# Layer 0's latent attention units in two groups of six and four key tiles

## Chip, core and metric

The kernel runs on one core of a Trainium2 chip. The metric is the device time of one execution in microseconds (us). Every time below comes from runs of the kernel before, or from one profiled execution of it. The engines are named as the profile names them: PE (TensorE, matrix products; PEld is its loading of weights), DVE (VectorE), ACT (ScalarE), POOL (GpSimd) and SP (SyncE, which here issues DMAs).

## What is computed

Two attention layers run over 1024 latent tokens and 256 context tokens of width 1024. Layer 0 is grouped-query attention with 16 query heads of width 64 over 4 key and value heads; layer 1 is a latent attention. The change touches layer 0 alone:

```python
def gqa_attend(q, k, v):
    s = jnp.einsum('bqhgd,bkhd->bhgqk', q, k).astype(jnp.float32) * (GQA_HEAD_DIM ** -0.5)
    p = jax.nn.softmax(s, axis=-1).astype(v.dtype)
    return jnp.einsum('bhgqk,bkhd->bqhgd', p, v)
...
    k_all = jnp.concatenate([kc, k], axis=1)
    v_all = jnp.concatenate([vc, v], axis=1)
    o = sweep_query_blocks(lambda qb: gqa_attend(qb, k_all, v_all), q).reshape(B, S, GQA_WIDTH)
...
    oc = gqa_attend(qc, kc, vc).reshape(B, L, GQA_WIDTH)
```

Latent queries read all 1280 keys (ten tiles of 128), context queries only the 256 context keys (two tiles).

## The kernel before

**Units.** `Attention.run` walks over a list of units. A latent unit is one query head with its 1024 latent queries against ten key tiles. A context unit is one key head with its four query heads of 256 context queries against the last two key tiles. Layer 0 has 20 units, counted from 0 here: latent ones, with context units at places 4, 9, 18 and 19. Unit 17 is the last latent one.

**A unit.** For each key tile, `scores_by_halves` (L492) multiplies keys by queries in two halves of 512 queries, which run side by side in the two halves of PE's rows. A tile is four products per half: high part by high part, low by high, high by low, and a product with the constant `minus` that subtracts a shift of each query (`shift`). The scores go to a PSUM buffer `st`, of which there are two. ACT takes the exponential (L508) into `p`, a pair of tiles to a buffer, five buffers in all, just those of one unit. Then `do_av` (L546) multiplies all value tiles by the exponentials into the one PSUM buffer `av`, and `finish` copies it to `os` on ACT (L576).

**Sums for the softmax.** The exponentials of a unit are added up over its tiles. POOL adds whole tiles (`acp`, L542). DVE first adds the two tiles of a pair for the last two pairs (`pair_sum`, `acd`, L528), which POOL adds on top. The `total` of a unit (L597, products with `twos`) sums over the partitions on PE; DVE transposes and inverts it (L601, L602). It is put on a list and runs one unit later, ahead of that unit's value products. The reciprocals go out to memory and come back spread over partitions (`rrow`, `rb`), POOL multiplies them with the gate (L616) and the result with both (L617), and `od` is stored.

**The shift.** Each query's shift is the maximum over its approximate scores. These maxima are made units ahead: with every score tile two steps of maxima are issued, products on PE (L393, L403) into one of three PSUM buffers `mx`, and reduces on DVE (L395, L404). A latent unit has 20 such steps, the last four for the context keys. 28 steps are done when unit 0 starts, so in most latent units the last step for the next latent unit falls on the sixth tile. Then DVE reduces once more (L416), and a `turn` is put on a list: PE transposes the row (L422), DVE copies it to `crow` (L424), and SP copies it into `shift` by DMA (L427). `run_turns` issues what is on this list, before the change once per unit, behind its tenth score tile.

**Order.** PE, DVE and ACT run in the order in which the code issues (`manual_schedule` in `run`). POOL and SP are put in order by the compiler's scheduler, each a queue that runs in its order. The weights for the output projection are loaded in pieces, one behind every second unit, with casts on ACT (L157) and subtractions on POOL (L136, `wb`).

**The groups.** A group is a run of key tiles whose scores are issued together and whose value products follow. `cut` is zero for all units but the last latent one, so a unit is one group there:

```python
                    cut = 6 if u is self.last_lat else 0
                    ...
                    for group in (kts[:cut], kts[cut:]):
                        ...
                        self.run_turns()
                        ...
                        while self.totals:
                            self.totals.pop(0)()
                        ...
                        self.do_av(u, group, ps)
```

Of the kernel before, what the change touches and what calls it, by code (L numbers as in the profile page):

```python
# [36 lines left out]
def hybrid_kernel(ctx: ExitStack, tc: tile.TileContext, ins: dict, out: bass.AP):  # L37
# [197 lines left out]
    class Plan:  # L235
# [8 lines left out]
        def run(self):  # L244
            engines = mybir.EngineType
            with tc.manual_schedule(engines={engines.PE, engines.Activation, engines.DVE, engines.Pool, engines.SP}):
                for _, _, fn, args in sorted(self.todo, key=lambda e: e[:2]):
                    fn(*args)
# [60 lines left out]
    class Attention:  # L309
# [319 lines left out]
        def run(self, lead, ahead, extra, tail):  # L629

            count = lead
            parts = None
            with tc.manual_schedule(engines={mybir.EngineType.PE, mybir.EngineType.DVE, mybir.EngineType.Activation}):
                for t, u in enumerate(self.units):
                    kts = u["kts"]
                    for v in self.units[t:t + 2]:
                        self.load_v(v)
                    while self.started < min(t + 1 + ahead, len(self.units)):
                        self.start_unit()
                    whole = len(kts) > 4  # L640
                    cut = 6 if u is self.last_lat else 0

                    def one_more():
                        nonlocal count
                        count += 1
                        self.maxima(count, t + 1 + ahead)

                    for group in (kts[:cut], kts[cut:]):
                        if not group:
                            continue  # L650
                        end = group[-1] == kts[-1]
                        final = t == len(self.units) - 1 and end
                        p2s = [self.pp.tile([P, 2, 1024], F32, name="p", tag="p", bufs=5) for _ in range(len(group) // 2)]
                        ps = [p2[:, a, :] for p2 in p2s for a in range(2)]

                        late = not whole and t >= len(self.units) - 2
                        n1 = len(ps) - (4 if whole and end else 2 if late else 0)
                        for i, kt in enumerate(group):
                            self.run_deferred(self.step)
                            if HALVES[self.l]:  # L660
                                count += 2
                                self.scores_by_halves(u, kt, ps[i], self.next_maxima(count, t + 1 + ahead))
                            else:
                                self.do_scores(u, kt, ps[i], one_more)
                            self.step += 1
                            if i < n1:
                                self.add_up(u, [ps[i]], [])
                        if end and t + 2 < self.started:
                            self.state[id(self.units[t + 2])].pop("rest", lambda: None)()
                        if final:  # L670
                            tail()
                        self.run_turns()
                        if late or final:
                            self.add_up(u, [], ps[n1:])
                        elif n1 < len(ps):
                            sums = [self.pair_sum(p2) for p2 in p2s[n1 // 2:]]
                            self.add_up(u, *(([], sums) if cut else (sums, [])))
                        if final:
                            self.run_deferred(self.step + 2)
                        while self.totals:  # L680
                            self.totals.pop(0)()
                        if t % 2 and end:
                            if parts:
                                parts()
                            parts = extra.pop(0)() if extra else None
                        self.do_av(u, group, ps)
                        self.step += (2 + len(group)) // 3
                while self.totals:
                    self.totals.pop(0)()
            self.run_deferred(self.step)  # L690
# [600 lines left out]
    units = []  # L1291
# [8 lines left out]
    for g, pos in ((0, 4), (1, 9), (3, 18), (2, 19)):  # L1300
        units.insert(pos, ctxu[g])

    at = Attention(0, units, dict(scale=0.125, load=l0_load, scores=l0_scores, maxima=l0_maxima, mparts=1, open=l0_open, kbufs=2, qbufs=3, vw=256))
    stE = ExitStack()
    with tc.tile_pool(name="wkg0a", bufs=4, **right) as wkg:
        for m in range(2, 4):
# [286 lines left out]
    units = []  # L1593
    for p_ in range(8):
        for par in range(2):
            h = 2 * p_ + par
            units.append(dict(kind="lat", h=h, pair=p_, par=par, vg=(h // 4, 128 * (h // 2 % 2)), vc=64 * par,
                              kts=list(range(TT))))
    at = Attention(1, units, dict(scale=float(96 ** -0.5), load=l1_load, scores=l1_scores, maxima=l1_maxima, mparts=2, open=l1_open, open_late=l1_open_late,
                                  kbufs=3, qbufs=3, vw=128))  # L1600
    stE = ExitStack()

# [197 lines left out]
```

## Time and profile before

| | |
|---|---|
| median of 3 runs | 1709.44 us (1705.8 to 1714.31) |
| the profiled execution | 1707.59 us, of which the span of the program is 1705.8 |
| granted clock of PE, mean | 0.996 |
| attention of layer 0 | from about 372 to 752 us of the span |
| attention of layer 1 | from about 1197 to 1616 us |

The span is cut into 40 slices in the page; each digit is the busy share of a slice in tenths:

```profile
PE   8999999999999999999989999999999999999998
DVE  3765552357778777625675657754677777777231
ACT  4642221124445544432244533340434444344310
POOL 2763431218789988743245544350668787787511
PEclk9999999999999999999999999999999999999999
```

A slice is 42.6 us, so the attention of layer 0 fills the tenth to the eighteenth. The costliest groups of instructions that the change touches, with busy time, the mean length of one in ns, the idle time of the engine before them, and what ended it:

```profile
L508 ACT ACTIVATE p<-st 128x1024 f32<-128x1024 f32 x328 | 336.0, 1027 | 169.8 <-PE st L501 134.8
L542 POOL TENSOR_TENSOR acp<-acp,p 128x1024 f32<-128x1024 f32 x128 | 305.8, 2389 | 7.8
L555 PE MATMUL av<-p,v 128*64 128x512 f32 x1312 | 289.9, 595 | 0.0
L528 DVE TENSOR_REDUCE acd<-p 128x512 f32<-128x1024 f32 x124 | 144.7, 1220 | 7.9 <-ACT p L508 7.8
```

These counts are of both layers; layer 1 has units of the same shape.

### The profile page before, as it was taken

The numbers are of one execution on the slowest core, as the hardware profiler recorded it, in microseconds if no ns is written. First come the engines' busy times: TensorE is split into PE (matmuls) and PEld (weight loads), VectorE is DVE, ScalarE is ACT, GpSimd is POOL, SyncE is SP. The second block draws the span as 40 slices with busy tenths as digits, with TensorE's granted clock in tenths as the row PEclk, the third lists the DMA queues.
The fourth block names the chain that finished last, engine by engine and source line by source line (L and its number), as shares of the span: only waits on it lengthen the run. The fifth ranks groups of instructions, "written<-read, shape, count | busy, mean of one in ns | idle before, by whom it ended". The sixth has DMA issues, their size and how long they took to land. (4 is left out here: it accounts for less than half of the span.)

```text
span 1705.8 us, 27449 instructions
## 1 busy us (share of the span) xinstructions
PE 1667.9 (98%) x10244; PEld 1196.9 (70%) x10244; DVE 1046.6 (61%) x1807; ACT 645.1 (38%) x943; POOL 961.4 (56%) x646
## 2 busy tenths in 40 slices
PE   8999999999999999999989999999999999999998
PEld 5776778775555555557878898986767667667587
DVE  3765552357778777625675657754677777777231
ACT  4642221124445544432244533340434444344310
POOL 2763431218789988743245544350668787787511
PEclk9999999999999999999999999999999999999999
DMA  9557754521242422146433766766565655653452
GB/s 315 169 150 241 253 176 142 152 81 45 63 121 61 112 63 63 38 137 204 139 94 117 233 189 182 207 192 164 135 137 134 134 122 121 146 124 91 125 160 74
DMA packets 219821, 238.97 MB, mean 140 GB/s; under 512 B 23016, under 2 KB 159192, under 8 KB 219688
## 3 DMA queue, kind: packets, MB, share of 16 engines
q1 hardware_dynamic: 219264, 237.11, 49.5%
q8 instruction: 81, 1.33, 0.3%
q14 instruction: 52, 0.43, 0.1%
q10 hardware_dynamic: 424, 0.11, 0.0%
HBM read 163.37 MB, written 73.63 MB: 139 GB/s over the span
## 5 line engine op out<-in xcount | busy, mean ns | idle before, releaser
L395 DVE TENSOR_REDUCE m<-mx 128x1 f32<-128x512 f32 x512 | 336.2, 687 | 176.3 <-PE mx L393 170.5
L508 ACT ACTIVATE p<-st 128x1024 f32<-128x1024 f32 x328 | 336.0, 1027 | 169.8 <-PE st L501 134.8
L542 POOL TENSOR_TENSOR acp<-acp,p 128x1024 f32<-128x1024 f32 x128 | 305.8, 2389 | 7.8
L555 PE MATMUL av<-p,v 128*64 128x512 f32 x1312 | 289.9, 595 | 0.0
L555 PEld LDWEIGHTS av<-p,v 128*64 128x64 f32 x1312 | 90.9, 137 | 180.6 <-issue 177.9
L542 POOL TENSOR_TENSOR acp<-p 128x1024 f32<-128x1024 f32 x34 | 81.4, 2396 | 148.0 <-ACT p L508 147.9
L542 POOL TENSOR_TENSOR acp<-acp,acd 128x1024 f32<-128x1024 f32 x60 | 142.2, 2370 | 22.3 <-DVE acd L528 19.1
L528 DVE TENSOR_REDUCE acd<-p 128x512 f32<-128x1024 f32 x124 | 144.7, 1220 | 7.9 <-ACT p L508 7.8
L136 POOL TENSOR_TENSOR wb<-wraw,wa 128x512 fp32r<-128x512 f32 (+3 forms) x73 | 95.4, 1326 | 81.2 <-ACT wa L157 81.2
L93 PE MATMUL mm<-wa,hh 128*128 128x512 f32 (+2 forms) x336 | 127.4, 379 | 1.1 <-ACT hh L890 1.1
L501 PE MATMUL st<-QH,KH 64*128 64x512 f32 x320 | 122.2, 404 | 1.0 <-DVE gth L303 1.0
L95 PE MATMUL mm<-wa,hl 128*128 128x512 f32 (+2 forms) x336 | 121.5, 362 | 1.6 <-DVE hl L893 1.6
L94 PE MATMUL mm<-wb,hh 128*128 128x512 f32 (+2 forms) x336 | 121.2, 361 | 0.0
L501 PE MATMUL st<-QH,KL 64*128 64x512 f32 x320 | 119.0, 392 | 0.0
L501 PE MATMUL st<-QL,KH 64*128 64x512 f32 x320 | 118.3, 390 | 0.0
L576 ACT COPY os<-av 128x512 f32<-128x512 f32 x36 | 21.1, 587 | 255.9 <-PE av L555 205.9
L93 PE MATMUL y<-wa,oh 128*128 128x512 f32 (+1 forms) x296 | 114.1, 386 | 1.4 <-DVE yt L750 1.4
L95 PE MATMUL y<-wa,ol 128*128 128x512 f32 (+1 forms) x296 | 113.5, 384 | 0.0
L94 PE MATMUL y<-wb,oh 128*128 128x512 f32 (+1 forms) x296 | 113.5, 383 | 0.0
L404 DVE TENSOR_REDUCE m<-mx 128x2 f32<-128x512 f32 x144 | 95.4, 688 | 24.0 <-PE mx L403 18.9
L393 PE MATMUL mx<-KH,QH 64*128 64x512 f32 x256 | 102.7, 405 | 0.5 <-DVE m L404 0.3
L93 PE MATMUL mm<-hh,wa 128*128 128x512 f32 x256 | 102.0, 399 | 0.5 <-ACT th L86 0.5
(240 smaller groups left out, 4023.1 us busy)
## 6 DMA issues: line engine op xcount, KB each, us to landing
mraw<-in_l_w_mod SPq DMA_DIRECT2D x64, 256.0 KB
wraw<-in_l_w_in SPq DMA_DIRECT2D x28, 512.0 KB
KH<-k1h SPq DMA_DIRECT2D x32, 320.0 KB
KL<-k1l SPq DMA_DIRECT2D x32, 320.0 KB
rb<-rrow SPq DMA_DIRECT2D x72, 128.0 KB
mraw<-in_l_w_mod SPq DMA_DIRECT2D x16, 512.0 KB
sgd<-gth SPq DMA_DIRECT2D x32, 256.0 KB
wraw<-in_l_w_out SPq DMA_DIRECT2D x16, 512.0 KB
```

The lines of the kernel that those rows point to most:

```text
L93: pe.matmul(ps, lhsT=lh(k), rhs=rh(k), start=first and i == 0, stop=False)
L94: pe.matmul(ps, lhsT=lh(k), rhs=rl(k), start=False, stop=False)
L95: pe.matmul(ps, lhsT=ll(k), rhs=rh(k), start=False, stop=last and i == len(ks) - 1)
L136: eng.tensor_sub(lo, a, b)
L393: pe.matmul(held["m"][:, cs], lhsT=q[:, t * P:(t + 1) * P], rhs=k[:, ks], start=j == 0, stop=j == len(pairs) - 1)
L395: dve.reduce_max(s["m"][:, i, n:n + 1], held["m"], axis=AX.X)
L404: dve.reduce_max(s["m"][:, 2 * i:2 * i + 2, 2 if u["kind"] == "lat" else 0], m.rearrange("p (a b) -> p a b", a=2), axis=AX.X)
L501: pe.matmul(ps[:, n * 512:(n + 1) * 512], lhsT=lh, rhs=rh, start=j == 0, stop=j == last)
L508: act.activation(p, ps, AF.Exp, scale=self.ops["scale"])
L528: dve.reduce_sum(t[:, ns], p2.rearrange("p a n -> p n a")[:, ns, :], axis=AX.X)
L542: pool.tensor_add(t, a, b)
L555: pe.matmul(s["av"][64 * n:64 * n + 64, :], lhsT=s["v"][:, kt, u["vc"]:u["vc"] + 64], rhs=p[:, n * 512:(n + 1) * 512], start=kt == kts[0], ...
```

## The change

`Attention` takes a number `cut` with its operations, 6 for layer 0 and 0 for layer 1. Every latent unit of layer 0 but the last is then issued as two groups, tiles 0 to 5 and tiles 6 to 9: scores, values, scores, values. In each of the two groups the last pair of exponentials is summed by DVE (`n1 = len(ps) - 2`) and handed on to POOL as a part; before, it was the last two pairs of the unit. The totals of earlier units are issued only in a unit's second group. The last latent unit, the context units and layer 1 keep what they had. Turns are still issued behind every group.

```diff
-                    cut = 6 if u is self.last_lat else 0
+                    lastl = u is self.last_lat
+                    cut = 6 if lastl else self.ops["cut"] if whole else 0
...
-                        n1 = len(ps) - (4 if whole and end else 2 if late else 0)
+                        if cut and not lastl:
+                            n1 = len(ps) - 2
+                        else:
+                            n1 = len(ps) - (4 if whole and end else 2 if late else 0)
...
-                            self.add_up(u, *(([], sums) if cut else (sums, [])))
+                            self.add_up(u, *(([], sums) if lastl else (sums, [])))
...
-                        while self.totals:
+                        while self.totals and (end or lastl):
...
-    at = Attention(0, units, dict(scale=0.125, load=l0_load, scores=l0_scores, maxima=l0_maxima, mparts=1, open=l0_open, kbufs=2, qbufs=3, vw=256))
+    at = Attention(0, units, dict(scale=0.125, load=l0_load, scores=l0_scores, maxima=l0_maxima, mparts=1, open=l0_open, cut=6, kbufs=2, qbufs=3, vw=256))
...
-    at = Attention(1, units, dict(scale=float(96 ** -0.5), load=l1_load, scores=l1_scores, maxima=l1_maxima, mparts=2, open=l1_open, open_late=l1_open_late,
+    at = Attention(1, units, dict(scale=float(96 ** -0.5), load=l1_load, scores=l1_scores, maxima=l1_maxima, mparts=2, open=l1_open, cut=0, open_late=l1_open_late,
```

The order of PE in unit 1 before, from the last context maximum of the sixth tile to the seventh tile, and at the unit's end:

```order
L403 MATMUL mx<-KA,QH 128x256 x2
L501 MATMUL st<-QL,KA 128x512
L501 MATMUL st<-shift_2949,minus 128x512
L501 MATMUL st<-QL,KA 128x512
L501 MATMUL st<-shift_2949,minus 128x512
L393 MATMUL mx<-KA,QH 128x512
L501 MATMUL st<-QH,KA 128x512 x2
```

```order
L393 MATMUL mx<-KA,QH 128x512
L501 MATMUL st<-QL,KA 128x512 x2
L501 MATMUL st<-shift_2949,minus 128x512 x2
L422 MATMUL mx<-ident,m_3829 8x128
L597 MATMUL mx<-acp,twos 32x256 x4
L555 MATMUL av<-p,v 64x512 x20
```

The same two places with the change:

```order
L403 MATMUL mx<-KA,QH 128x256 x2
L501 MATMUL st<-QL,KA 128x512
L501 MATMUL st<-shift_2949,minus 128x512
L501 MATMUL st<-QL,KA 128x512
L501 MATMUL st<-shift_2949,minus 128x512
L422 MATMUL mx<-ident,m_3826 8x128
L555 MATMUL av<-p,v 64x512 x12
L393 MATMUL mx<-KA,QH 128x512
L501 MATMUL st<-QH,KA 128x512 x2
```

```order
L393 MATMUL mx<-KA,QH 128x512
L501 MATMUL st<-QL,KA 128x512 x2
L501 MATMUL st<-shift_2949,minus 128x512 x2
L597 MATMUL mx<-acp,twos 32x256 x4
L555 MATMUL av<-p,v 64x512 x8
```

The turn (L422) has moved from behind the tenth tile to behind the sixth, and twelve of the twenty value products (L555) with it; the total (L597) still stands behind the tenth. Such a place is found in 13 units; in units 3 and 8 the turn stays at the unit's end.

DVE in the same unit, from the first maxima of the unit to the reciprocal, before:

```order
L395 TENSOR_REDUCE m<-mx 128x1 x8
L404 TENSOR_REDUCE m<-mx 128x2 x4
L416 TENSOR_REDUCE m_3829<-m 128x8
L395 TENSOR_REDUCE m<-mx 128x1 x8
L424 CAST crow<-mx 8x128
L528 TENSOR_REDUCE acd<-p 128x512 x4
L601 STREAM_TRANSPOSE mx<-mx 128x256
L602 RECIPROCAL cr<-mx 128x8
```

and with the change:

```order
L395 TENSOR_REDUCE m<-mx 128x1 x8
L404 TENSOR_REDUCE m<-mx 128x2 x4
L416 TENSOR_REDUCE m_3826<-m 128x8
L424 CAST crow<-mx 8x128
L528 TENSOR_REDUCE acd<-p 128x512 x2
L395 TENSOR_REDUCE m<-mx 128x1 x8
L528 TENSOR_REDUCE acd<-p 128x512 x2
L601 STREAM_TRANSPOSE mx<-mx 128x256
L602 RECIPROCAL cr<-mx 128x8
```

The copy of the turn now follows L416 directly, and half of the pair sums stands ahead of the last eight maxima.

POOL in unit 3 and into the context unit behind it, before:

```order
L542 TENSOR_TENSOR acp<-p 128x1024
L616 TENSOR_TENSOR rb<-rb,sg 128x512
L617 TENSOR_TENSOR os<-os,rb 128x512
L542 TENSOR_TENSOR acp<-acp,p 128x1024 x4
L136 TENSOR_TENSOR wb<-wraw,wa 128x512 x2
L542 TENSOR_TENSOR acp<-acp,acd 128x1024 x2
L616 TENSOR_TENSOR rb<-rb,sg 128x512
```

and with the change:

```order
L616 TENSOR_TENSOR rb<-rb,sg 128x512
L542 TENSOR_TENSOR acp<-p 128x1024
L617 TENSOR_TENSOR os<-os,rb 128x512
L542 TENSOR_TENSOR acp<-acp,p 128x1024 x2
L542 TENSOR_TENSOR acp<-acp,acd 128x1024
L542 TENSOR_TENSOR acp<-acp,p 128x1024 x2
L136 TENSOR_TENSOR wb<-wraw,wa 128x512 x2
L542 TENSOR_TENSOR acp<-acp,acd 128x1024
```

The product with the reciprocals (L616) now stands ahead of the unit's first add, and the weight pieces (L136) ahead of its last one only.

## The prediction

> **What bounds the kernel now.** I read the page first, then the stretch that the change touches.
>
> ```profile
> span 1705.8 us, 27449 instructions
> PE 1667.9 (98%) x10244; PEld 1196.9 (70%) x10244; DVE 1046.6 (61%) x1807; ACT 645.1 (38%) x943; POOL 961.4 (56%) x646
> ```
>
> PE is busy for 98% of the span. The windows view of the attention of layer 0 (371 to 753 us), and of 8 us inside it, agrees; its columns are length, busy time by engine, granted clock, DMA share and GB/s.
>
> ```profile
> core 0: us, PE busy (x) PEld busy (x) DVE busy (x) ACT busy (x) POOL busy (x), PEclk, DMA share, GB/s
> 371.00:753.00 382.00, 379.28 (x2617) 210.18 (x2616) 280.57 (x442) 189.53 (x199) 319.39 (x155) 1.00 0.28 75
> 460.00:468.00 8.00, 7.30 (x56) 3.68 (x51) 4.12 (x8) 3.23 (x4) 4.79 (x3) 1.00 0.35 100
> ```
>
> PE is idle for 2.7 of 382 us. A change that only reorders PE's own work has almost nothing to win there, and every new wait that lands on PE is paid in full. The timeline of one latent unit on PE (number 5, counted from 0) shows what a unit is made of. Columns: start, length, engine, line, operation, names, sizes, count.
>
> ```profile
> 466.50 0.50 PE L393 MATMUL mx<-KA,QH 64*128 64x512 f32 x1
> 467.77 0.61 PE L501 MATMUL st<-QH,KA 64*128 64x512 f32 x2
> 469.14 0.50 PE L501 MATMUL st<-QH,KA 64*128 64x512 f32 x2
> ...
> 473.00 0.39 PE L501 MATMUL st<-QH,KA 64*128 64x512 f32 x2
> ...
> 473.58 0.28 PE L403 MATMUL mx<-KA,QH 64*128 64x256 f32 x1
> ...
> 478.18 0.39 PE L501 MATMUL st<-QH,KA 64*128 64x512 f32 x2
> ...
> 479.43 0.27 PE L422 MATMUL mx<-ident,m 128*8 128x128 f32 x1
> 479.63 0.64 PE L597 MATMUL mx<-acp,twos 128*32 128x256 f32 x8
> 480.20 8.80 PE L555 MATMUL av<-p,v 128*64 128x512 f32 x40
> 488.94 0.50 PE L393 MATMUL mx<-KA,QH 64*128 64x512 f32 x1
> ```
>
> Ten score tiles take 12.93 us (466.50 to 479.43), the transpose of the next shift (L422, "the turn") 0.20, the total of the unit before (L597) 0.57, the ten value tiles 8.74; a unit is 22.44 us. The last tile, from its first score product at 478.18 to the turn, takes 1.25. The sixth tile starts at 473.00, so with nothing to wait for, a turn could stand behind it at 474.25.
>
> DVE in the same unit, and ACT's last two exponentials of it:
>
> ```profile
> 467.04 4.98 DVE L395 TENSOR_REDUCE m<-mx 128x1 f32<-128x512 f32 x8 [1.56 <-PE mx L393]
> 471.94 2.68 DVE L404 TENSOR_REDUCE m<-mx 128x2 f32<-128x512 f32 x4
> 474.65 0.18 DVE L416 TENSOR_REDUCE m<-m 128x8 f32<-128x24 f32 x1
> ...
> 479.95 4.68 DVE L528 TENSOR_REDUCE acd<-p 128x512 f32<-128x1024 f32 x4
> 484.56 0.44 DVE L601 STREAM_TRANSPOSE mx<-mx 128x256 f32<-128x256 f32 x1
> 485.04 0.21 DVE L602 RECIPROCAL cr<-mx 128x8 f32<-128x8 f32 x1
> ```
>
> ```profile
> 478.44 2.12 ACT L508 ACTIVATE p<-st 128x1024 f32<-128x1024 f32 x2 [0.46 <-PE mx L393]
> ```
>
> L416 makes the row that the turn transposes. It ends at 474.83, which is 4.6 us before the turn needs it now, and 0.58 after the end of the sixth tile.
>
> **The change, part by part.** First, the turn moves into a wait. The list of pending turns is run behind each group. In 13 of the 15 changed units (all but 3 and 8, where by the program's order L416 follows later tiles) the turn therefore stands behind the sixth tile, and the value products of group one stand behind it in PE's order. Nothing on DVE ahead of L416 changes, so it still ends 8.33 us after the unit's start. What it takes to hand over to PE I read from a total that waited for an add of Pool:
>
> ```profile
> 459.19 4.82 POOL L542 TENSOR_TENSOR acp<-acp,acd 128x1024 f32<-128x1024 f32 x2
> 464.07 0.64 PE L597 MATMUL mx<-acp,twos 128*32 128x256 f32 x8 [0.70 <-POOL acp L542]
> ```
>
> The add ended at 464.01 and PE started 0.06 later. For DVE I take 0.1, between 0.05 and 0.2. PE thus stands 0.58 + 0.1 = 0.68 us at the end of group one. At the unit's end nothing is won for it: the turn started there without a wait on PE, and its 0.20 only moves. Behind the waiting turn stand twelve value products and then the second scores, for which ACT, DVE and Pool wait in turn.
>
> Second, the value products come in two runs. The last latent unit is cut 6 + 4 already:
>
> ```profile
> 727.29 5.37 PE L555 MATMUL av<-p,v 128*64 128x512 f32 x24
> 732.59 0.50 PE L501 MATMUL st<-QH,KA 64*128 64x512 f32 x2
> ...
> 737.00 3.65 PE L555 MATMUL av<-p,v 128*64 128x512 f32 x16
> 740.59 0.50 PE L501 MATMUL st<-QH,KA 64*128 64x512 f32 x2
> ```
>
> From each start to the next scores it takes 5.30 and 3.59 us, together 8.89 against 8.74: +0.15 for one more end of a run.
>
> Third, the score pipeline starts once more per unit. PE writes scores into two PSUM buffers that ACT must empty. The waits view of the attention of layer 0 (total, times, longest):
>
> ```profile
> PEld st L501 <- ACT p L508: 22.6, 67, 0.7
> ...
> PE st L501 <- ACT p L508: 0.8, 3, 0.3
> ...
> POOL rb L616 <- DMA rb<-rrow: 27.3, 9, 4.7
> ```
>
> The weight loads wait 67 times, 0.34 us each, some four times per unit. PE itself hardly waits: tile 1 lasts from 467.77 to 469.14, which is 1.37 with such a wait behind it, and the last tile 1.25 without. A wait costs PE about 0.1, not 0.34. A group starts with both buffers free, so I expect two waits in six tiles and one in four, three for four. Ten tiles were 12.93; six are 7.75 (473.00 - 466.50 + 1.25), and four 5.14 (tile 3 starts one tile of 1.25 behind the 2.64 of the first two, and then 1.25): 12.89, a gain of 0.04.
>
> A changed unit: 0.68 + 0.15 - 0.04 = +0.79, 13 times that is +10.3. Units 3 and 8 have only the other two terms, +0.11 each, +0.2.
>
> Fourth, the pair sums: two per unit before and after, and seven adds on Pool. DVE's sum of tiles 4 and 5 falls into the first value run. Its exponential ends about 1.1 us behind the sixth tile (480.56 against 479.43 at the unit's end), the sum takes half of 4.68, and the run lasts 5.30. The sum of 8 and 9 and the reciprocal (0.44, 0.21) end 4.3 us behind the scores; the next unit's first maximum reaches DVE 0.57 + 3.59 + 0.54 = 4.7 us behind them. So these cost nothing, with 0.4 to spare; were that cover gone, each unit would lose the difference.
>
> Fifth, the shift's copy leaves earlier. In unit 6, PE waited for it:
>
> ```profile
> 490.40 0.68 PE L501 MATMUL st<-shift,minus 64*128 64x512 f32 x2 [0.27 <-DMA shift<-crow]
> ...
> 492.26 0.51 PE L501 MATMUL st<-QH,KA 64*128 64x512 f32 x2
> ```
>
> Tile 2 starts 3.32 us after the unit there, and 2.64 in unit 5. The copy now leaves half a unit earlier; the stores and loads ahead of it on SP wait for Pool's L617 until some 10 us into the unit, and 13 are left then: -0.7.
>
> Sixth, the context units. Units 4 and 9 are two tiles long, and the total of the unit before stands close behind them. Pool decides there:
>
> ```profile
> 620.23 0.64 PE L597 MATMUL mx<-acp,twos 128*32 128x256 f32 x8
> ...
> 630.97 1.29 POOL L616 TENSOR_TENSOR rb<-rb,sg 128x512 f32<-128x512 f32 x1 [2.91 <-DMA rb<-rrow]
> ...
> 633.59 2.40 POOL L542 TENSOR_TENSOR acp<-p 128x1024 f32<-128x1024 f32 x1
> 636.07 9.77 POOL L542 TENSOR_TENSOR acp<-acp,p 128x1024 f32<-128x1024 f32 x4
> ...
> 456.74 2.50 POOL L136 TENSOR_TENSOR wb<-wraw,wa 128x512 fp32r<-128x512 f32 x2
> ```
>
> The reciprocals come back to Pool (L616) 10.7 us behind a total. With the shorter pair sum it is 9.4, and the next unit now starts 4.16 behind the total instead of 9.31, so L616 moves from 1.4 to 5.2 us into a unit. From there L616 and L617 (2.6), six adds (14.7), in unit 3 the two weight pieces (2.5) and the last add (2.4) end at 27.4. The total in unit 4 could start at 22.55 + 2.6 = 25.2. It waits 2.2, against 0.70 before: +1.5, between 0 and +5 by the time of that DMA. Unit 8 has no weight pieces ahead of its last add and just fits: 0.
>
> The sum is 10.3 + 0.2 - 0.7 + 1.5 = +11.3 us. The profiled execution took 1707.59 us (1.8 of it around the span), 1.85 under the median of 1709.44. From the one I get 1718.9, from the other 1720.7, and take 1720.
>
> **The rivals.** The score pipeline pays it back: if each wait of the weight loads is worth its 0.34 to PE, the one that goes gives 15 x 0.34 = 5.1, and +6 is left: 1715.5, inside 0.5% (8.5 us, about what a measurement of this kernel can tell from no change). For it speaks the row of 22.6 us, against it the row of 0.8.
>
> Faster, at the same place: ACT catches up in both pauses, so that only two of 4.2 waits stay in each unit (15 x 2.2 x 0.34 = -11.2), and the turn does not stand. With -0.7 that is 1697.5. It decides when L416 ends before the sixth tile does, 0.6 us earlier than now. Against it: the last context maximum leaves PE at 473.86 and its reduce starts at 473.94, so DVE has no backlog that it could lose. The Trainium skill ("Perfetto Trace Analysis", "Optimization Strategy") says that where the most contended engine changes between regimes, interleaving them may help, which is what this change does with scores and values; here the trace has PE as the busiest in both.
>
> Pool falls behind: L616 now stands 5 us into a unit, ahead of most adds. If the reciprocals' DMA comes 3 to 4 us later still, units 4 and 9 wait 4 to 5 us more each: +20, 1729. That wait was up to 4.7 us before, all of it on Pool and none on PE.
>
> The clock: if the short stalls cost PE its clock, so that each first value run went at half speed, 13 x 5.3 = 69 us would come on top: 1789. Against it, the window from 460 to 468 holds the stall of 0.70 us, and the granted clock is 1.00 there. The Trainium skill ("TensorE: Matmul & The Clock Gate", "A second HAM failure mode: psum-queue depth-cycling") tells of a kernel whose frequent micro-idles made the clock oscillate; this trace does not show that.
>
> No effect: L416 is in time after all and the rest cancels, 1709.5.
>
> **How the numbers follow.** The forecast has 0.55 (0.45 of it over 0.5%, 0.10 just below), the pipeline that pays back 0.21, no effect 0.05, faster 0.06, Pool behind 0.11, the clock 0.02. So slower 0.58, within 0.5% 0.36, faster 0.06. The range leaves out the faster rival, the clock and most of Pool's: from 1710 (no effect) to 1727 (a handing over of 0.2, 13 x 0.1 more, and 5 us in unit 4).
>
> **What would show it.** In the profile after: L422 behind six tiles in 13 units, with PE idle before it for 0.6 to 0.8 us and released by DVE L416; units of 23.2 us; L555 in runs of 5.3 and 3.6; no wait for the shift; the total in unit 4 waiting some 2 us for Pool. I am wrong if PE stands there for less than 0.3 us, if units get shorter than 22.4, or if the wait falls on another engine than DVE.

## The result, and the profile after

The changed kernel took 1720.88 us (median of 5 runs, 1718.88 to 1726.7), the kernel before 1708.13 us (5 runs on the same chip). The ratio is 1.0073, with a 95% interval from 1.0056 to 1.009: slower by 0.7%, some 12.5 us. The profiled execution took 1718.88 us. Lines up to L638 keep their numbers; those of `run` stand 1 to 4 later.

The page's totals of the changed kernel first:

```profile
span 1717.1 us, 27480 instructions
PE 1669.7 (97%) x10244; PEld 1199.1 (70%) x10244; DVE 1050.1 (61%) x1807; ACT 644.4 (38%) x943; POOL 959.2 (56%) x646
```

PE does the same 10244 products in nearly the same busy time, 1669.7 against 1667.9 us, and the span has grown by 11.3 us. So most of the loss is idle time on PE. The windows view of the stage (length, busy times, granted clock, DMA share, GB/s), and the waits view of it cut down to PE itself (total, times, longest) with the two rows that stood in the prediction:

```profile
371.00:764.00 393.00, 381.11 (x2612) 211.79 (x2611) 283.70 (x441) 189.42 (x199) 317.77 (x154) 1.00 0.26 72
```

```profile
POOL rb L616 <- DMA rb<-rrow: 41.9, 14, 6.2
...
PEld st L501 <- ACT p L508: 13.7, 48, 0.7
...
PE mx L422 <- DVE m L416: 8.4, 13, 0.7
...
PE mx L597 <- POOL acp L542: 1.6, 1, 1.6
...
PE st L501 <- ACT p L508: 0.8, 3, 0.3
PE st L501 <- DMA shift<-crow: 0.6, 1, 0.6
```

PE is idle for 11.9 of 393 us, where it was 2.7 of 382. One row holds 8.4 of it: the turn waits for DVE's L416 in 13 units. The row in which the weight loads wait for ACT is the other lesson: it fell from 22.6 us to 13.7, and PE won nothing by it. PE's own row of that wait is 0.8 us before and after.

One unit on PE (number 5, as before) shows where the wait stands. Start, length, engine, line, operation, names, count, and in brackets the idle time ahead of it and what ended it:

```profile
469.50 0.50 PE L393 MATMUL mx<-KA,QH 64*128 64x512 f32 x1
...
477.97 0.27 PE L422 MATMUL mx<-ident,m 128*8 128x128 f32 x1 [0.66 <-DVE m L416]
478.17 5.37 PE L555 MATMUL av<-p,v 128*64 128x512 f32 x24
483.47 0.49 PE L393 MATMUL mx<-KA,QH 64*128 64x512 f32 x1
...
488.58 0.64 PE L597 MATMUL mx<-acp,twos 128*32 128x256 f32 x8
489.15 3.65 PE L555 MATMUL av<-p,v 128*64 128x512 f32 x16
492.74 0.50 PE L393 MATMUL mx<-KA,QH 64*128 64x512 f32 x1
```

The unit lasts from 469.50 to 492.74, 23.24 us, where it was 22.44. DVE in it:

```profile
477.65 0.18 DVE L416 TENSOR_REDUCE m<-m 128x8 f32<-128x24 f32 x1
...
492.62 0.21 DVE L602 RECIPROCAL cr<-mx 128x8 f32<-128x8 f32 x1
493.27 4.98 DVE L395 TENSOR_REDUCE m<-mx 128x1 f32<-128x512 f32 x8 [0.44 <-PE mx L393]
```

L416 ends at 477.83 and the turn starts at 477.97. DVE's sums and the reciprocal end 0.44 us before the next maximum is there for it.

### The profile page after: what moved, and what is told of

The parts are those of the page before. It is cut to its first block, busy times and chain, and to the rows that moved or that the text cites. A ratio compares the mean times of both kernels' runs of the same rounds, so it can differ in the third digit from the quotient of the medians.

```text
span 1717.1 us, 27480 instructions
## 1 busy us (share of the span) xinstructions
PE 1669.7 (97%) x10244; PEld 1199.1 (70%) x10244; DVE 1050.1 (61%) x1807; ACT 644.4 (38%) x943; POOL 959.2 (56%) x646
## 5 line engine op out<-in xcount | busy, mean ns | idle before, releaser
L395 DVE TENSOR_REDUCE m<-mx 128x1 f32<-128x512 f32 x512 | 336.2, 688 | 161.6 <-PE mx L393 157.5
L542 POOL TENSOR_TENSOR acp<-acp,p 128x1024 f32<-128x1024 f32 x128 | 304.9, 2382 | 12.5 <-ACT p L508 5.6
L555 PE MATMUL av<-p,v 128*64 128x512 f32 x1312 | 293.2, 596 | 0.0
L555 PEld LDWEIGHTS av<-p,v 128*64 128x64 f32 x1312 | 89.5, 137 | 174.8 <-issue 169.9
L542 POOL TENSOR_TENSOR acp<-acp,acd 128x1024 f32<-128x1024 f32 x60 | 142.5, 2375 | 22.6 <-DVE acd L528 19.4
L136 POOL TENSOR_TENSOR wb<-wraw,wa 128x512 fp32r<-128x512 f32 (+3 forms) x73 | 95.8, 1332 | 79.7 <-ACT wa L157 79.7
L95 PE MATMUL mm<-hh,wb 128*128 128x512 f32 x256 | 101.2, 395 | 0.0
```

The lines of the kernel that those rows point to most:

```text
L95: pe.matmul(ps, lhsT=ll(k), rhs=rh(k), start=False, stop=last and i == len(ks) - 1)
L136: eng.tensor_sub(lo, a, b)
L395: dve.reduce_max(s["m"][:, i, n:n + 1], held["m"], axis=AX.X)
L542: pool.tensor_add(t, a, b)
L555: pe.matmul(s["av"][64 * n:64 * n + 64, :], lhsT=s["v"][:, kt, u["vc"]:u["vc"] + 64], rhs=p[:, n * 512:(n + 1) * 512], start=kt == kts[0], ...
```

## The experiments

The theory: the loss is the turn, which since the change has to wait for a reduce that ends behind the sixth tile. The rivals: the split into two groups costs the time itself (value runs, restarts, pair sums, Pool's later start), or the wait only marks a place where something else would stand anyway. The table collects all runs. A regular unit is the commonest latent unit, from its first product to the next unit's; the stage runs from the first score product of unit 0 to the end of unit 19. Both are differences of start times on PE's timeline in the profiled execution. The ratio comes from several runs of each kernel, and it does not follow the stage to the microsecond: e1, e2, e4, e5, e7 and e9 grew by 2 to 7 us more than their stage did. The rest of the program differs between single executions by as much (last section), and where that difference lies is open.

| kernel | regular unit | unit 4 | unit 9 | stage | ratio to before |
|---|---|---|---|---|---|
| before | 22.44 | 5.69 | 4.97 | 378.9 | 1 |
| changed | 23.24 | 6.64 | 4.93 | 390.7 | 1.0073 (1.0056 to 1.009) |
| e1, maxima earlier | 22.53 | 6.64 | 6.23 | 381.3 | 1.0026 (1.0014 to 1.0039) |
| e2, turn at the unit's end | 22.55 | 5.57 | 4.96 | 392.7 | 1.0094 (1.0075 to 1.0114) |
| e3, only the turn moved | 23.09 | 4.95 | 4.97 | 385.9 | 1.0035 (1.0022 to 1.0049) |
| e4, cut 4 and 6 | 22.52 | 5.97 | 4.97 | 380.1 | 1.0027 (1.0013 to 1.0041) |
| e5, pair sums late | 23.69 | 8.76 | 6.09 | 398.0 | 1.0138 (1.0116 to 1.016) |
| e6, weight pieces later | 23.24 | 4.93 | 6.33 | 389.4 | one run |
| e7, e1 and e6 together | 22.5 | 4.93 | 6.89 | 381.3 | 1.0029 (1.0015 to 1.0044) |
| e8, before, turn moved, maxima earlier | 22.37 | 4.96 | 4.93 | 376.3 | 0.9984 (0.9972 to 0.9995) |
| e9, changed, slower reduce | 24.10 | 5.97 | 4.93 | 402.5 | 1.0178 (1.0158 to 1.0199) |

**e1: the maxima two steps earlier.** If the turn waits because L416 comes too late, two steps of maxima more in advance put L416 ahead of the sixth tile's end, and nothing else of the change is taken back.

```diff
-    at.run(28, 3, pieces, lambda: first.extend(fetch_first(0, 2)))
+    at.run(30, 3, pieces, lambda: first.extend(fetch_first(0, 2)))
```

> The changed kernel with the maxima of layer 0 two steps (one key tile) further ahead: 30 done before unit 0 instead of 28. The turn stays behind the sixth tile in the same 13 units, but L416 now follows the fifth tile's maxima and should end some 1.2 us earlier, before the sixth tile ends. Theory (PE stands at the turn for L416): L416 is done when the turn comes, 13 x 0.73 = 9.5 us come back, 1711 to 1712, and units of 22.5 us. Rival (splitting the unit itself costs 0.8 us, by two value runs, pair sums or the restart of the scores): stays at 1720 to 1721 with units of 23.2 us. Rival (Pool and its DMA): the 13 units stay and only units 4 and 11 change.

It took 1711.99 us. The longest of PE's own waits in the stage:

```profile
PE mx L597 <- POOL acp L542: 2.8, 2, 1.6
```

The row of the turn is gone, and the units are 22.53 us long. Of the 11.8 us that the stage had lost, 9.4 came back. What is left is mostly 0.1 a unit and two waits for Pool. By the ratios, some 8 of 12.5 us came back.

**e3: only the turn moved.** The other side of e1: the kernel before, unsplit, with the turns run behind the sixth tile.

```diff
+                            if i == 5 and not self.l:
+                                self.run_turns()
```

> The kernel before, not split, with the turn of layer 0 issued behind the sixth tile of a unit (and again at its end for what is left). Theory (the wait for L416): PE stands there 0.6 to 0.7 us in 13 units, of which the next wait for ACT at the seventh tile may give back 0.1: +7.5 to +9, 1716 to 1717. Rival (the split itself): no change, 1708.

It took 1715.03 us. The longest of PE's own waits:

```profile
PE mx L422 <- DVE m L416: 8.4, 13, 0.7
```

The row of the changed kernel stands there word for word, in a kernel without its split. The unit grows by 0.65. The time grew a little less than expected, since the waits of unit 4 for Pool (0.70) and of unit 6 for the shift went away: 13 x 0.65 - 0.7 - 0.7 = 7.1, and the stage grew by 7.0.

**e9: the reduce made longer.** In the changed kernel L416 is issued five times in layer 0 instead of once; the four more write the same result.

```diff
-                dve.reduce_max(m, s["m"], axis=AX.X)
+                for _ in range(1 if self.l else 5):
+                    dve.reduce_max(m, s["m"], axis=AX.X)
```

> The changed kernel with the shift's transpose on VectorE (L416) issued five times instead of once in layer 0, the last of the five the one that the turn waits for; each is about 0.18 us, so the turn may start 0.7 to 0.9 us later. Theory (the turn is bound by the end of L416 in each of the 13 units): the wait of L422 for L416 grows from 0.65 to 1.35 to 1.5 us a unit, regular units from 23.24 to 23.9 to 24.1 us, and the time by 9 to 12 us, to 1730 to 1733 us. Rival (the wait is the way through the semaphore or another wait that ends at the same time, and the added work lies beside it): units stay at 23.24 to 23.4 us; 1721 to 1723 us.

It took 1737.1 us. The reduces on DVE and the turn on PE, which stand one line later in this kernel:

```profile
484.40 1.03 DVE L417 TENSOR_REDUCE m<-m 128x8 f32<-128x24 f32 x5
```

```profile
485.58 0.27 PE L423 MATMUL mx<-ident,m 128*8 128x128 f32 x1 [1.49 <-DVE m L417]
```

The five end at 485.43, and the turn starts 0.15 later, as it did behind one. It now waits 1.49 us instead of 0.66, and the unit is 24.10 us, 0.86 longer. So each 0.85 us that DVE adds to L416 comes back on PE in full in the regular units. Units 3 and 8, where the turn stands at the unit's end, grew by 0.7 each too, in part by waits for DVE's later reduces (L395): the longer L416 holds up more than the turn, and this run does not keep the two apart. The stage grew by 11.8, within what was expected; the median grew by 16, outside. In the profiled execution the stage started at 375.7 us, against 371.6 in the changed kernel, ahead of any turn of it. That accounts for most of the rest in that execution. Why it was late there, and whether it was in the others, was not settled.

**e4: cut four and six.** Behind four tiles L416 has not been issued yet, so the turn stays behind the tenth.

```diff
-    ... open=l0_open, cut=6, kbufs=2, qbufs=3, vw=256))
+    ... open=l0_open, cut=4, kbufs=2, qbufs=3, vw=256))
```

> The changed kernel cut 4 + 6 instead of 6 + 4. The turn's row is still made behind the sixth tile, which now is the second of group two, so the turn comes at the unit's end with no wait. Theory (the wait for L416): like e2, 1711 to 1712. Rival (the split itself, in whichever place): 1720. If the shorter second group of 6 + 4, with only 3.6 us of values over DVE's last pair sum, cost something, this one would be faster than e2; I expect the same within 1 us.

It took 1714.38 us, some 2.5 us above the expectation, which the stage (1.2 us over before) does not show; the ratio is that of e1. No wait of a turn is left, and units are 22.52 us. Two groups in another proportion, without the turn's wait, cost the same 0.1 a unit.

**e2: the turn back to the unit's end.** This looked like the plainest way to undo the loss, and missed.

```diff
-                        self.run_turns()
+                        if end:
+                            self.run_turns()
```

> The changed kernel with turns issued only behind the second group of a unit, as before the change; the split stays. Theory (the wait for L416): 9.5 us come back, 1711 to 1712; units of 22.55 us, that is 0.1 above the 22.44 of before, all of it from the second value run. Rival (the split itself): 1720 to 1721. In the first case the cost of the split alone is the rest over before, about 15 x 0.1 plus the wait for Pool in unit 4: 2 to 3 us.

It took 1725.37 us, more than the changed kernel. The turn's wait is gone, and most units are 22.55 us long, as expected. But two new rows have come:

```profile
PE st L501 <- DMA shift<-crow: 5.4, 2, 3.0
PE mx L393 <- DVE cr L602: 2.0, 2, 1.1
```

For the first, SP's issues in unit 5 (start, length, what is issued) and the product that needs the shift:

```profile
485.22 1.08 SPq L621 DMA_DIRECT2D od<-os  x2
...
489.64 1.34 SPq L427 DMA_DIRECT2D shift<-crow  x2
```

```profile
492.79 0.69 PE L501 MATMUL st<-shift,minus 64*128 64x512 f32 x2 [2.34 <-DMA shift<-crow]
```

The turn is at the unit's end as before the change, but only the total and four value tiles (0.57 + 3.59 us) lie between it and the next unit, instead of all ten (0.57 + 8.74). The copy to `shift` stands in SP's queue behind stores and loads, and comes 2.3 us and more too late. Units 6 and 11 are 26.49 and 28.13 us long. For the second row, DVE at the end of unit 2:

```profile
433.17 0.28 DVE L424 CAST crow<-mx 8x128 fp32r<-8x128 f32 x1
436.58 0.28 DVE L424 CAST crow<-mx 8x128 fp32r<-8x128 f32 x1 [3.14 <-DMA shift<-crow]
...
439.57 0.21 DVE L602 RECIPROCAL cr<-mx 128x8 f32<-128x8 f32 x1
```

Two turns come together there. There is one `crow`, so the second copy waits 3.14 us for the DMA of the first, and the pair sum and the reciprocal stand behind it on DVE. The next unit started at 437.51, and its maxima wait for a buffer until L602 has read it; units 3 and 8, both with such a wait, are 23.64 and 23.70 us long. A second `crow` was not tried. So with a cut at six a turn at the unit's end comes too late in these units for what hangs on it; what helps is e1's earlier L416.

**e5: both pair sums in the second group.** This takes away the cover that the fourth step of the prediction counted on.

```diff
-                            n1 = len(ps) - 2
+                            n1 = len(ps) - (4 if end else 0)
```

> The changed kernel with both pair sums of a unit in its second group (tiles 6 and 7, 8 and 9; DVE sums nothing in the first group). PE's order is that of the changed kernel. Theory (DVE's sum in the second value run was covered with 0.4 us to spare, and no more): DVE's two sums now end some 5.9 us behind the scores, 1.2 us after the next unit's first maximum is ready; the maxima and L416 come 1.2 us later, all of which PE pays, at the maxima or at the turn: units of 24.4 us, 15 x 1.2 = 18 us over the changed kernel, 1737 to 1740. Rival (DVE has room there, PE's waits come from the turn's place alone): within 2 us of the changed kernel.

It took 1729.93 us: slower, but by 9 us and not by 16 to 19. DVE at the end of a unit, and PE at the start of the next:

```profile
639.13 4.68 DVE L528 TENSOR_REDUCE acd<-p 128x512 f32<-128x1024 f32 x4
...
644.22 0.21 DVE L602 RECIPROCAL cr<-mx 128x8 f32<-128x8 f32 x1
```

```profile
643.00 0.50 PE L393 MATMUL mx<-KA,QH 64*128 64x512 f32 x1
...
644.58 0.47 PE L393 MATMUL mx<-KA,QH 64*128 64x512 f32 x1
```

DVE is 1.4 us behind the unit's start. PE does not stand for that long: with three `mx` buffers it makes two maxima before the third has to wait. The first tile lasts 1.58 us instead of 1.27, and the turn waits 0.78 instead of 0.65, as DVE catches up with most of it by then. That makes 0.44 in most units and nothing in units 5 and 10 (23.2 us); the longer units 4 and 9 (8.76 and 6.09 us) give most of the rest. The mechanism is the expected one, at little more than a third of the price that was set on it. That the three buffers take the difference is read from these rows; no run has another number of them.

**e6 and e7: the weight pieces later.** In unit 3 Pool has two pieces of a weight ahead of the add that unit 4's total waits for. Here they are put off to later units, in the changed kernel (e6) and in e1 (e7).

```diff
-                        if t % 2 and end:
+                        if t % 2 and end and (self.l or t > 4):
```

> The changed kernel with layer 0's weight pieces started behind unit 5 instead of unit 1, so that none stands ahead of Pool's last add in unit 3. Theory (the total in unit 4 waits for Pool, which the pieces make late): the wait of 1.6 us in unit 4 goes, that unit takes 5.0 instead of 6.6; the pieces reach unit 9 then, and if they stand ahead of the last add in unit 8 or 9, a wait of up to 2 us shows up there. One look: read from the profile, the time within noise of the changed kernel.

> e1 and e6 together: turns without a wait, and no weight pieces before unit 5. Best version that the theory offers of a split kernel: units of 22.53 us, no wait for the shift, less wait for Pool in unit 4. The split itself still costs 0.1 us a unit, 1.4 us; 0.7 of unit 6 and 0.7 of unit 4 come back against the kernel before. 1708 to 1711: no better than before, since PE has nothing left to win there.

They took 1721.56 us (one run) and 1713.37 us. In e6 unit 4 is 4.93 us, without a wait; the row of the waits is now this, and it stands in unit 9, which grew from 4.93 to 6.33:

```profile
PE mx L597 <- POOL acp L542: 1.3, 1, 1.3
```

The pieces were the cause of unit 4's wait, but putting them off moves most of it. In e7, unit 9 waits 1.9 us and the shift comes 0.7 us late in unit 6, where no wait was expected. The time is 2 us above the expectation, and by ratio e7 is no better than e1.

**e8: the kernel before, with the turn moved and the maxima earlier.** The two useful edits without the split.

```diff
+                            if i == 5 and not self.l:
+                                self.run_turns()
...
-    at.run(28, 3, pieces, lambda: first.extend(fetch_first(0, 2)))
+    at.run(30, 3, pieces, lambda: first.extend(fetch_first(0, 2)))
```

> Before's unsplit scores and values and its pair sums, with only the turn moved behind the sixth tile and the lead of the maxima raised from 28 to 30. Theory (the 0.65 us a unit that the changed kernel loses is the turn waiting for the shift's transpose, which a turn two matmuls later no longer does): the turn's wait for L416 is gone, units of 22.4 to 22.5 us, unit 4 at 4.95 and unit 6 at 22.4 to 22.7 us; 1706 to 1709 us, within 0.2% of before. Rival (the turn's place costs by itself): units of 23.1 us as in e3_turn_only; 1715 us.

It took 1704.47 us (12 runs), 1.5 us below the expectation, against 1708.21 before (17 runs): 0.9984, with an interval that ends at 0.9995. PE's own waits in the stage are one row:

```profile
PE st L501 <- ACT p L508: 1.0, 4, 0.3
```

The waits for Pool (0.70, unit 4) and for the shift (0.7, unit 6) of the kernel before are gone, and a regular unit is 0.07 us shorter: 0.7 + 0.7 + 13 x 0.07 = 2.3 of the 2.6 us by which the stage is shorter. What makes the 0.07 is open. This is the fastest of the kernels here, by less than 0.2%. Against e1, which differs from it only by the split, it shows what the split costs with no turn waiting: 381.3 - 376.3 = 5.0 us, of which units 4 and 9 hold 1.7 and 1.3, and 13 units 0.16 each the rest.

## Why the prediction was right

The forecast of 1720 us came from +11.3 us; the stage grew by 11.8. The bulk of the forecast is right by its mechanism. That the sums agree to half a microsecond is in part luck, since the fifth step came out 1.0 us above its forecast and the sixth 0.6 below. Step by step:

| step | forecast, us | measured, us |
|---|---|---|
| turn waits for L416, 13 units | 0.68 each | 0.65 each |
| two value runs and a restart, the same units | +0.11 each | +0.15 each |
| the same in units 3 and 8 | +0.11 each | +0.05 each |
| pair sums | 0, with 0.4 to spare | 0, with 0.44 to spare |
| shift's copy | -0.7 | +0.3 |
| unit 4; unit 9 | +1.5; 0 | +0.95; -0.04 |

**First, the turn.** It was the bulk of the loss, by the mechanism forecast: e3 brings it about alone, e1 takes it away alone, and e9 makes it longer by what it adds to DVE. The handing over from DVE to PE, put at 0.1, was 0.14; PE reached the turn a little later than reckoned, so the wait was 0.65 and not 0.68.

**Second and third, value runs and restarts.** From 478.17 to 483.47 and from 489.15 to 492.74 are 5.30 and 3.59 us, to the hundredth those of the last latent unit that they were read from. The restart gains next to nothing, as forecast.

**Fourth, the pair sums.** They are covered, with 0.44 us left. That each unit would lose the difference without that cover was too simple: e5 went 1.4 us over, and lost 0.44.

**Fifth, the shift's copy: wrong.** Unit 6 lost its wait as forecast, it grew by 0.1 where its neighbours grew by 0.8. But unit 11 got one, and is 24.23 us long. L617 on POOL, in units 5 and 10:

```profile
486.68 1.29 POOL L617 TENSOR_TENSOR os<-os,rb 128x512 f32<-128x512 f32 x1
...
582.55 1.29 POOL L617 TENSOR_TENSOR os<-os,rb 128x512 f32<-128x512 f32 x1
```

SP in unit 5, behind it in unit 10, and PE in unit 11:

```profile
489.82 1.32 SPq L427 DMA_DIRECT2D shift<-crow  x2
```

```profile
583.86 1.08 SPq L621 DMA_DIRECT2D od<-os  x2
584.99 0.60 SPq L1252 DMA_DIRECT2D KA<-k0h  x1
585.64 1.23 SPq L1252 DMA_DIRECT2D KB<-k0l  x2
586.97 1.33 SPq L427 DMA_DIRECT2D shift<-crow  x2
```

```profile
591.86 0.71 PE L501 MATMUL st<-shift,minus 64*128 64x512 f32 x2 [0.55 <-DMA shift<-crow]
```

The prediction named this queue and this wait, but put the end of L617 some 10 us into the unit, with 13 left. It ends at 487.97, 18.5 us into unit 5, and at 583.84, 17 us into unit 10 (which starts at 566.89): behind a context unit two results are finished in one unit, and the copy stands behind the store of the second. Some 5 to 6 us were left. In unit 5 the copy was issued at 489.82 and came in time; in unit 10 it was issued as long ahead of the next unit, 586.97 against 590.12, and came too late. There three loads of keys stand right ahead of it.

How long the copy is under way can be read from the updates of its semaphore in the traces, from the issue of its first half to the last update. It is 2.4 us in unit 5 of the changed kernel, with no key load right ahead of it, 3.2 us with one (unit 5 of e9), 4.2 with two (unit 5 of e3) and 4.9 with three (unit 10 here and in e6). In e6 the same three stand ahead, but the copy was issued at 584.58, 5.3 us ahead of the next unit, and unit 11 is 23.26 us long, without a wait. No run changed these loads alone.

So the step failed in two things. The end of L617 lies where it was put, 9.7 to 10.1 us into the unit, in units 2, 3, 7, 8 and 13 to 16, and later, 11.9 to 18.5 us, in units 5, 6 and 10 to 12, which follow the context units. And the time that the copy is under way behind key loads was not reckoned.

**Sixth, the context units.** Pool decides in unit 4 as forecast, with this row ahead of the total:

```profile
464.64 2.38 POOL L542 TENSOR_TENSOR acp<-acp,acd 128x1024 f32<-128x1024 f32 x1
```

Unit 3 started at 440.36 on PE. The last add ends 26.7 us into it (27.4 forecast). The total waited 1.60 us instead of 2.2: the term was right in kind and 0.55 too large. Unit 9 had no wait, as forecast, but no slack left either: in e1, e6 and e7 it waits.

**The rivals.** The pipeline that pays back needed the weight loads' waits to be worth their length to PE. They fell by 8.9 us, and PE's own row stayed at 0.8. The faster rival needed L416 ahead of the sixth tile's end; e1 and e8 are that case, and with the split it is still slower than before. The Trainium skill ("Perfetto Trace Analysis", "Optimization Strategy") holds that interleaving may help where the most contended engine changes between regimes; with the turn out of the way the split still cost 5.0 us of the stage here, and PE was the busiest in both regimes. Pool fell behind on itself, where L616's wait for its DMA went from 27.3 to 41.9 us, but only the 1.6 us in unit 4 reached PE. The clock stayed: 1.00 over the stage, with its 13 stalls. The oscillation that the Trainium skill tells of ("TensorE: Matmul & The Clock Gate", "A second HAM failure mode: psum-queue depth-cycling") does not show in this trace.

## What to carry to other kernels

When groups are split, look for small steps that are issued "behind each group": they move too, and one that waits for another engine can land where its input isn't there yet. Read the end of that input against the new place before and after, to a tenth of a microsecond; here 0.65 us in 13 units made 8.4 of the 11.8 us lost. And where the engine that bounds the kernel is 98% busy, first look at its few waits: e8, which removes most of them, is the one kernel here that is faster than before, by 0.16%.

## What the runs showed of the chip

- From the end of a reduce on DVE to the start of the product on PE that waits for it were 0.14 to 0.15 us; from an add on POOL, 0.05 to 0.06.
- Waits of the weight loads (PEld) overstate what PE loses: 22.6 us against 13.7, with 0.8 us on PE in both.
- The copy to `shift` was under way for 2.4 us with no key load right ahead of it in its queue, and for 3.2, 4.2 and 4.9 us with one, two and three.
- The part of the program ahead of the layer's attention, which none of the edits was aimed at, ended between 370.8 and 375.7 us in the profiles of the eleven kernels. What follows the stage took 953.3 to 963.3 us. A single execution therefore can't tell 4 us; the intervals above come from up to 28 runs a side.
